# Two units of the first projection take turns over the token tiles while the norm goes on

## The chip, the cores and the metric

One NeuronCore of a Trainium2 chip runs the whole computation in one launch. The metric is the device time of one execution in microseconds. All work is in 32-bit floating point; a product of two such matrices is made of three matmuls of halves (high times high, high times low, low times high), which is why every weight and activation is split into a high and a low part.

## The reference, cut to what matters

Two layers over 1024 latent tokens and 256 context tokens (T = 1280), 1024 channels each. What concerns the change is the beginning of a layer:

```python
mod_x = (silu_c @ w_ada[l] + b_ada[l])[:, None, :]        # likewise mod_c from c_ctx
sh1_x, sc1_x, gt1_x, sh2_x, sc2_x, gt2_x = jnp.split(mod_x, 6, axis=-1)
hx = modulate(rms_norm(x, g_norm1[l]), sh1_x, sc1_x)      # likewise hc from ctx
qa, ka, va, qb, kb, vb, qc, kc, vc = jnp.split(hx @ w_in[l], bounds, axis=-1)
# then: QK norm of every head, rotary positions on q and k of groups A and C,
# three kinds of attention, output projection with gate gt1, ConvFFN with sh2, sc2 and gate gt2
```

`rms_norm` divides a token by the root of its mean square and multiplies by a gain; `modulate(h, shift, scale)` is `h * (1 + scale) + shift`. The modulation vectors of a layer are six pieces of 1024; the kernel makes them in three pieces of 2048 columns.

## The kernel before, in words

Activations lie with channels on the partitions: eight tiles X[k] of 128 channels by 1280 tokens. Instructions are issued in an order written out by hand in Python generators; each engine works through its own part of that order, and semaphores hold it where an operand is not there yet. The order of the program is therefore also the order of each engine's queue, and of the DMA queue of SyncE, which loads weights and tables.

The first norm of a layer (`FirstNorm`) goes over the tokens in five pieces of 256. A piece needs its sum of squares (`squares`, in layer 1 the loop `last`), a statistics step (`norm_stat`: TensorE sums over the channels at L226, VectorE adds the epsilon at L229, GpSimd takes the power at L230), a cast (`norm_cast`, L237: TensorE spreads the factor over 128 partitions), and eight steps of `norm_apply`, one for each X[k]: VectorE scales (L255), ScalarE writes the high part (L274, or L271 and L272), VectorE or GpSimd the low part (L263 or L260). `SPREAD` and `SPREAD1` say which steps give the low part to GpSimd.

The projection `inproj` has six units of 384 columns (two of kind A, two of C, two of B) and, in each unit, ten tiles of 128 tokens: 60 slots. It runs unit 0 over all ten tiles, then unit 1, and so on. In slot s:

- `stage1(s)`: 24 matmuls into `acc` (L398), ScalarE's square of the result (L403), the copy of v (L407), VectorE's sum over each head (L413, L415), GpSimd's power (L416);
- `stage2(s-1)`: VectorE multiplies by the root (L430), GpSimd multiplies by the cosine table or the gain (L440, L445), VectorE by the sine table (L445);
- the rotary add of slot s-2 (L452), and `stage3(s-2)`: TensorE's transposes into `pt` (L463, L465), ScalarE's and VectorE's copies into `sg` (L472, L474, L475), DMA to memory (L478).

Ahead of each slot stands `bg(s)`. In slots 0 to 7 it issues squares and norm steps (counts in `Q_ST`, `P_ST`, `P_ST1`), enough that the piece a slot reads is complete; `STAT0`, `CAST0` and their like place statistics and casts behind a slot's matmuls. At slot 8 it closes the norm's buffers and sets up the remaining modulation pieces (three in layer 0, two in layer 1), whose weights (L1370) go into the space of X[k], free once the norm has read it; the pieces run from slot 9 on, two small steps every second slot (`hold`). From slot `S_FIRST` on, the first operands of the attention are loaded and cast (`attention_first`, L513 and on).

A unit's weights are four raw loads of 384 KB (`load`, L348), each split into high (ScalarE, L103) and low (VectorE, L104) by `split`. Four raw buffers and six split buffers exist; `split(n)` also issues the load n + 4. `weights` splits the next unit's first two in its slots 2 and 4 of ten, `weights_done` the other two behind the last slot.

Of the kernel before, what the change touches and what calls it, by code (L numbers as in the profile page):

```python
# [14 lines left out]
F32 = mybir.dt.float32  # L15
F32R = mybir.dt.float32r
# [7 lines left out]
KT = D // 128  # L24
# [3 lines left out]
CH = [(0, 512), (512, 512), (1024, 256)]  # L28
NP = 8
NPT = 6  # L30
Q_PRE = [0, 0, 0, 2, 4, 3, 1, 1]
Q_ST = [1, 2, 4, 3, 0, 2, 0, 1, 0]
SQ_ENG = "vgv"
STAT0 = [0, 3, 3]
CAST0 = [1, 3, 4]
STAT1 = [0]
CAST1 = [1, 3, 5]
SPREAD = "vgvvgvvv"
SPREAD1 = "gvvvgvvv"
TST = [0, 0, 0, 0, 0, 0, 0, 0, 0, 0, 0, 0, 0, 0, 0, 0, 0, 2, 1, 0, 0, 0, 0, 1, 1, 0]  # L40
# [1 line left out]
T_CAST = [16, 17]  # L42
T_TAB = 10
T_SP = [0, 1, 1, 1]
P_ST1 = [4, 4, 4, 4, 4, 4, 4, 4]
P_ST = [1, 7, 1, 7, 5, 2, 5, 4]
STRETCH = 1.2
LEADL = 35
LEADB = 12
# [24 lines left out]
class Build:  # L74
# [126 lines left out]
    def squares(self, X, ss, sqp):  # L201

        nc = self.nc
        n = self.squared = 0
        for o in (512, 768, 1024):
            dst = ss[:, o - 512:o - 256]
            for k in range(KT):
                x = X[k][:, o:o + 256]
                if k == 0:
                    nc.scalar.activation(dst, x, AF.Square)  # L210
                else:
                    sq = sqp[:, 256 * (n % 2):256 * (n % 2) + 256]
                    n += 1
                    nc.scalar.activation(sq, x, AF.Square)
                    (nc.vector if SQ_ENG[o // 256 - 2] == "v" else nc.gpsimd).tensor_tensor(dst, dst, sq, op=ALU.add)
                self.squared += 1
                yield
# [93 lines left out]
    def ip_tables(self, l):  # L311

        nc, i = self.nc, self.i
        tp = self.iptab[1]
        self.ip_gains = gains = tp.tile([128, 320], F32, name=self.name("gains"))
        nc.sync.dma_start(gains[:], i["gains"][:, l, :])
        self.ip_tabs = {}  # L320
        for kd, off in (("A", 0), ("C", 256)):
            gd = GD[kd]
            h = gd // 2
            self.ip_tabs[kd] = cc, ss = [tp.tile([128, 2, 8, gd], F32, name=self.name(z + kd)) for z in ("cos", "sin")]
            for z, w in ((cc, "cos"), (ss, "sin")):
                nc.sync.dma_start(z[:, 1], i[w + kd][:])
            yield
            if kd == "A":
                for a, b in (("A", 0), ("B", 128), ("C", 256)):
                    z = gains[:, b + GD[a]:b + 2 * GD[a]]  # L330
                    nc.gpsimd.tensor_scalar(z, z, -math.sqrt(GD[a]), 1.0, op0=ALU.mult, op1=ALU.mult)
            g = gains[:, off:off + 2 * gd].rearrange("p (j d) -> p j d", d=gd)
            for j in range(2):
                nc.gpsimd.tensor_tensor(cc[:, j], cc[:, 1], g[:, j, :].unsqueeze(1).to_broadcast([128, 8, gd]), op=ALU.mult)
                for x, y in ((0, h), (h, 0)):
                    nc.gpsimd.tensor_tensor(ss[:, j, :, x:x + h], ss[:, 1, :, x:x + h],
                                            g[:, j, y:y + h].unsqueeze(1).to_broadcast([128, 8, h]), op=ALU.mult)
            yield

    def ip_loads(self, l):  # L340

        nc, i = self.nc, self.i
        raw, wts = {}, {}

        def load(n):
            if n < 24:
                w = self.ipraw[1].tile([128, 2, 384], F32, name=self.name("ipr"), tag="ipr", bufs=4)
                nc.sync.dma_start(w[:], i["win"][l, n // 4, :, 2 * (n % 4):2 * (n % 4) + 2, :])  # L348
                raw[n] = w

        def split(n):
            if n < 24:
                hi = self.ipw[1].tile([128, 2, 384], F32R, name=self.name("iph"), tag="iph", bufs=6)
                lo = self.ipw[1].tile([128, 2, 384], F32R, name=self.name("ipl"), tag="ipl", bufs=6)
                self.split(hi[:], lo[:], raw.pop(n)[:])
                wts[n] = (hi, lo)
                load(n + 4)

        def weights(u, t):
            if t in (2, 4):  # L360
                split(4 * u + 3 + t // 2)
            return [wts[4 * u + j] for j in range(4)]

        def weights_done(u):
            split(4 * u + 6)
            split(4 * u + 7)

        for j in range(4):
            load(j)
        self.ip_weights, self.ip_weights_done = weights, weights_done  # L370

        return split

    def inproj(self, l, H, bg, stat):
# [2 lines left out]
        tmpl = self.pool("iptmp")  # L377
        tmp, psp = tmpl[1], self.ipps[1]
        gains, tabs = self.ip_gains, self.ip_tabs
        slots = [(u, t) for u in range(6) for t in range(10)]  # L380
        state, vst = {}, {}

        def stage1(s):
# [8 lines left out]
            ws = self.ip_weights(u, t)  # L392
# [9 lines left out]
            sq = tmp.tile([128, 320], F32, name=self.name("sq"), tag="sq", bufs=1)  # L402
            nc.scalar.activation(sq[:, g0 * gd:W], acc[:, g0 * gd:W], AF.Square)  # L403
            nv = NV[kd]
            if t % 5 == 0:
                vst[u] = tmp.tile([128, 2, 5, 64], F32, name=self.name("vst"), tag="vst", bufs=2)
            nc.scalar.copy(vst[u][:, :nv, t % 5, :], acc[:, W:384].rearrange("p (v d) -> p v d", d=64))  # L407
            if t % 5 == 4:
                for j in range(nv):
                    dst = self.vs[l][self.vidx(u, j)][:, 64 * (t - 4):64 * (t - 4) + 320]  # L410
                    nc.scalar.dma_start(dst.rearrange("p (t d) -> p t d", d=64), vst[u][:, j, :, :])
            ss = tmp.tile([128, 8], F32, name=self.name("ss"), tag="ss", bufs=3)
            nc.vector.tensor_reduce(ss[:, g0:ng], sq[:, g0 * gd:W].rearrange("p (g d) -> p g d", d=gd), axis=AX.X,  # L413
                                    op=ALU.add)
            nc.vector.tensor_scalar(ss[:, g0:ng], ss[:, g0:ng], gd * EPS, None, op0=ALU.add)  # L415
# [39 lines left out]
        def stage3(s):  # L455
# [10 lines left out]
            qs = self.qs[l][u]  # L466

            def put(r, nb, src, c):
                sg = tmp.tile([128, 2, nb, 128], F32R, name=self.name("sg"), tag=f"sg{nb}", bufs=nb)
                hi, lo = (sg[:r, z].rearrange("p b n -> p (b n)") for z in range(2))  # L470
                if kd == "A":
                    nc.scalar.copy(f32(hi), src)  # L472
                else:
# [11 lines left out]
        for s in range(len(slots) + 2):  # L485
# [7 lines left out]
                stage3(s - 2)  # L493
            if 1 <= s <= len(slots):
                stage2(s - 1)
        self.close(tmpl, self.ipraw, self.iptab, self.ipw, self.ipps)

    @staticmethod
    def vidx(u, j):
# [636 lines left out]
    def run(self):  # L1136
# [19 lines left out]
        ss0 = sqp[1].tile([128, 512], F32, name="ss0")  # L1156
        ss = sqp[1].tile([128, 768], F32, name="ss")
        sqt = self.pool("sqt")
        squares = self.squares(X, ss, ss0)
# [33 lines left out]
        for l in range(L):  # L1193
# [12 lines left out]

            n_w = iter(range(1000))
            adw = lambda n_w=n_w: self.slot(f"x{next(n_w) % KT}")
            todo, hold = deque(), [True]
            first = self.attention_first(l)  # L1210
            lam = self.lambdas() if l == 0 else iter(())

            def bg(s, l=l, norm=norm, adw=adw, todo=todo, hold=hold, sqp=sqp, nps=nps, lam=lam, first=first, tables=tables):
                if s < 8:
                    nq, np_ = Q_ST[s] if l == 0 else 0, (P_ST, P_ST1)[l][s]
                    for j in range(max(nq, np_)):
                        if j < nq:
                            next(squares, None)
                        if j < np_:
                            norm.step()  # L1220
                    while norm.done < KT * (s // 2 + 1):
                        norm.step()
                elif s == 8:
                    self.close(sqp, self.ntl, nps)
                    which = [(a, b) for a, b in ((l, 1), (l, 2), (l + 1, 0)) if a < L]
                    loads = AdaLoads(self, adw, which, 1)
                    todo.extend(self.ada(a, b, loads, self.ipps[1]) for a, b in which)
                if s in (12, 16):
                    next(lam, None)
# [43 lines left out]
            def last(unit, spare, l=l, X=X, H=H, out=out):  # L1273
# [388 lines left out]
```

## Time and profile before

| what | value |
|---|---|
| runs shown | 3519.92, 3525.55 and 3526.09 us, median 3525.55 us |
| the profiled execution | 3518.43 us, span of its instructions 3516.7 us |
| TensorE busy in the span | 3381.2 us (96%) |
| VectorE, ScalarE, GpSimd busy | 2049.2, 1383.7 and 960.1 us |
| mean granted clock of TensorE | 0.988 |
| matmuls of the projection, layer 0 | from 38.0 us; slot 59 ends at 376.4 us |
| matmuls of the projection, layer 1 | from 1921.7 us; slot 59 ends at 2227.8 us |

Times in rows of the timeline are microseconds from the first instruction. A row gives start, duration, engine, line, operation, written and read tiles, shapes and count; in brackets stands how long the engine had been idle before it and what ended that. Matmuls overlap each other, so the duration of one is longer than the distance to the next. Rows with the letter q behind the engine (SPq, ACTq) are DMA instructions that the engine issues.

### The profile page before, as it was taken

Reading aid. Unit: us, or ns where it says so; the run is one execution under the profiler, and the core shown is the slowest. Engines: PE = TensorE matmul, PEld = TensorE weight load, DVE = VectorE, ACT = ScalarE, POOL = GpSimd, SP = SyncE. Lnnn points to the kernel's source line nnn. Section 1 sums busy time; section 2 is a strip of 40 time slices with the busy share of each in tenths; the row PEclk is TensorE's granted clock in tenths of the full one; section 3 lists DMA queues with packets and bytes.
Section 4 is the critical chain, followed back from the end, with each engine's and each line's share of the span. In section 5 each row is a group of like instructions: output and inputs, shape, how many; then the busy total and the mean of one; then the engine's idle time right before and its main releaser. Section 6 shows DMA issues by size and latency. Waiting matters only on the chain.

```text
span 3516.7 us, 55261 instructions
## 1 busy us (share of the span) xinstructions
PE 3381.2 (96%) x21808; PEld 2914.1 (83%) x21808; DVE 2049.2 (58%) x4167; ACT 1383.7 (39%) x2412; POOL 960.1 (27%) x863
## 2 busy tenths in 40 slices
PE   5899899999999999999999899999999999999999
PEld 3789788888888888888887789888888888888887
DVE  5544578776565544445446544587775645555555
ACT  4322478777332221122223322478775322222211
POOL 3444467755100000000002344467763100000000
PEclk8999999999999999999999999999999999999999
DMA  5563611220211111111112453512212111111112
GB/s 210 197 234 108 158 43 46 68 62 2 92 52 36 37 43 41 38 42 37 37 36 98 145 178 107 146 48 63 60 36 68 47 48 54 42 48 54 43 50 76
DMA packets 138084, 266.59 MB, mean 76 GB/s; under 512 B 15200, under 2 KB 76128, under 8 KB 137824
## 3 DMA queue, kind: packets, MB, share of 16 engines
q1 hardware_dynamic: 76880, 230.27, 21.1%
q10 hardware_dynamic: 60944, 32.78, 3.1%
q8 instruction: 172, 2.82, 0.3%
q14 instruction: 88, 0.72, 0.1%
HBM read 222.09 MB, written 40.89 MB: 75 GB/s over the span
## 4 chain that ended last, share of the span: by engine, by line
PE 83%; DVE 7%; POOL 4%; DMA 2%; issue 2%; ACT 2%; ACTq 0%; SPq 0%; DVEq 0%; POOLq 0%
PE psu L999 15%; PE psg L999 15%; PE dacc L1086 15%; PE acc L398 11%; PE T L783 6%; PE T L802 6%; PE S L676 5%; PE acc L935 4%; DVE P L694 2%; PE T L676 2%; POOL P L755 1%; PE ada L166 1%; POOL P L754 1%; DVE hl L263 1%; PE pt L463 1%
## 5 line engine op out<-in xcount | busy, mean ns | idle before, releaser
L1093 DVE SCALAR_TENSOR_TENSOR x<-dacc,mods,x 128x512 f32<-128x512 f32 (+1 forms) x440 | 303.8, 696 | 474.9 <-PE dacc L1086 474.8
L1086 PE MATMUL dacc<-ah,w 128*128 128x512 f32 (+1 forms) x1760 | 530.4, 369 | 2.1 <-DVE x L1093 1.6
L999 PE MATMUL psu<-hh,w 128*128 128x512 f32 (+1 forms) x1760 | 516.5, 368 | 1.1 <-ACT hh L274 1.1
L999 PE MATMUL psg<-hh,w 128*128 128x512 f32 (+1 forms) x1760 | 516.4, 368 | 0.0
L719 ACT ACTIVATE P<-P,sm 128x1280 f32<-128x1280 f32 (+3 forms) x360 | 434.6, 1209 | 122.0 <-DVE sm L694 99.8
L103 ACT CAST w<-wr 128x1024 fp32r<-128x1024 f32 x138 | 144.1, 1044 | 726.5 <-PE psg L999 538.5
L1086 PEld LDWEIGHTS dacc<-ah,w 128*128 128x128 f32 x1760 | 322.2, 188 | 61.1 <-DVE x L1093 4.5
L999 PEld LDWEIGHTS psu<-hh,w 128*128 128x128 f32 x1760 | 321.4, 189 | 56.5 <-ACT hh L274 1.3
L999 PEld LDWEIGHTS psg<-hh,w 128*128 128x128 f32 x1760 | 321.4, 189 | 55.5
L694 DVE CUSTOM_DVE_ANT_0 P<-S,small,sm 128x1024 f32<-128x1024 f32 x256 | 328.5, 1283 | 32.9 <-PE S L676 18.9
L398 PE MATMUL acc<-iph,hh 128*128 128x384 f32 (+1 forms) x960 | 334.6, 349 | 5.8 <-ACT iph L103 3.9
L398 PE MATMUL acc<-iph,hl 128*128 128x384 f32 (+1 forms) x960 | 323.4, 337 | 9.0 <-DVE hl L263 5.3
L999 PE MATMUL psu<-hl,w 128*128 128x512 f32 (+1 forms) x880 | 324.7, 369 | 0.1
L1086 PE MATMUL dacc<-al,w 128*128 128x512 f32 (+1 forms) x880 | 324.6, 369 | 0.0
L398 PE MATMUL acc<-ipl,hh 128*128 128x384 f32 (+1 forms) x960 | 323.0, 336 | 1.1 <-DVE ipl L104 1.1
L999 PE MATMUL psg<-hl,w 128*128 128x512 f32 (+1 forms) x880 | 324.0, 368 | 0.0
L783 PE MATMUL T<-ident,P 128*128 128x128 f32 x2400 | 313.5, 274 | 5.9 <-POOL P L755 5.5
L783 PEld LDWEIGHTS T<-ident,P 128*128 128x128 f32 x2400 | 270.8, 141 | 37.3 <-POOL P L755 12.0
L728 POOL TENSOR_SCALAR P<-P,sm 128x1280 f32<-128x1280 f32 (+3 forms) x216 | 248.1, 1151 | 181.4 <-DVE sm L726 116.7
L802 PE MATMUL T<-PT,v 128*64 128x128 f32 x4800 | 293.8, 276 | 3.5 <-DVE sm L836 3.0
L802 PEld LDWEIGHTS T<-PT,v 128*64 128x64 f32 x4800 | 259.6, 137 | 33.7 <-issue 14.7
L788 ACT COPY PT<-T 128x512 f32<-128x512 f32 (+1 forms) x461 | 246.7, 584 | 71.4 <-PE T L783 69.2
(195 smaller groups left out, 5612.9 us busy)
## 6 DMA issues: line engine op xcount, KB each, us to landing
wr<-in_wup SPq DMA_DIRECT2D x88, 512.0 KB, 3.5
x<-in_wada SPq DMA_DIRECT2D x80, 512.0 KB, 6.3
qs<-sg ACTq DMA_DIRECT2D x180, 128.0 KB, 1.8
wr<-in_wdown SPq DMA_DIRECT2D x44, 512.0 KB, 3.5
ipr<-in_win SPq DMA_DIRECT2D x48, 384.0 KB, 3.8
v<-vs SPq DMA_DIRECT2D x30, 320.0 KB, 3.2
hh<-qs SPq DMA_DIRECT2D x26, 320.0 KB, 6.2
x<-in_x SPq DMA_DIRECT2D x32, 256.0 KB, 4.4
```

Of the source, the lines that this page charges most:

```text
L103: self.nc.scalar.copy(hi, raw)
L398: nc.tensor.matmul(acc[:, c0:], lhsT=a[:, o:o + 128], rhs=b[:, k % 2, c0:], start=(k == 0 and a is hi and b is wh), stop=(k == KT - 1 and ...
L676: nc.tensor.matmul(S[:, pc:pc + w], lhsT=q[:K, 128 * t:128 * t + 128], rhs=k[:K, k0:k0 + w], start=(j == 0), stop=(j == len(ks) - 1))
L694: nc.vector.tensor_tensor_reduce(P[:, o:o + n], S[:, base:base + n], tab, op0=ALU.add, op1=ALU.min, scale=1.0, scalar=start, accum_out=sm[ ...
L719: nc.scalar.activation(P[:, :n], P[:, :n], AF.Exp, bias=sm[:, 0:1], scale=-1.0, accum_out=at())
L728: lambda e: nc.gpsimd.tensor_scalar(P[:, :n], P[:, :n], sm[:, 3:4], 1.0, op0=ALU.mult, op1=ALU.mult),
L783: nc.tensor.transpose(tp[:, 256 * x + 128 * hs:256 * x + 128 * hs + 128], P[hs][:, col[kt]:col[kt] + 128], self.ident[:])
L788: nc.scalar.copy(ts[:, :w], tp[:, :w])
L802: nc.tensor.matmul(O[64 * hs:64 * hs + 64, :128], lhsT=hds[hs]["v"][:, kt, :], rhs=ts[:, x + 128 * hs:x + 128 * hs + 128], start=(kt == kt ...
L999: nc.tensor.matmul(ps[:, o:o + n], lhsT=a[:, 128 * k:128 * k + 128], rhs=b, start=(k == 0 and a is wh and b is hi), stop=(k == KT - 1 and ...
L1086: nc.tensor.matmul(acc, lhsT=a[:, off:off + 128], rhs=b[:, o:o + n], start=(kk == 0 and a is wh and b is hi), stop=(kk == 1 and a is wl))
L1093: nc.vector.scalar_tensor_tensor(xs, acc, self.mods[l][:, 40 + m, v:v + 1], xs, op0=ALU.mult, op1=ALU.add)
```

## The change

Units 0 and 1 are in use at once. The first 20 slots alternate in pairs of token tiles:

`(0,0) (0,1) (0,2) (0,3) (1,0) (1,1) (0,4) (0,5) (1,2) (1,3) (0,6) (0,7) (1,4) (1,5) (0,8) (0,9) (1,6) (1,7) (1,8) (1,9)`

as (unit, token tile); units 2 to 5 follow as before. The five pieces of the norm are first read in slots 0, 2, 6, 10 and 14, where they were first read in slots 0, 2, 4, 6 and 8.

- The norm steps are spread over slots 0 to 13 (`S_NORM` = 14); the squares of layer 0 are nearly all issued beside the slots (three ahead of slot 0, 21 in slots 0 to 8; before, 11 ahead and 13 beside). Their scratch is the read part of X[0] and X[1].
- Unit 1's weights are split in slots 1 to 4, unit 2's in slots 16 to 19, the others at the old places. Eight split buffers for six; two raw buffers and, for weights 2 and 3, two more in a pool that is closed after their split; `split(n)` issues the load n + 2.
- The other modulation pieces are set up in slot 19 (`S_ADA`): the first load goes out in slot 20, the first matmuls stand in slot 24.
- The rotary table of kind C gets its own pool; it is loaded in slot 17 and multiplied by the gains in slot 20 (before: 9 and 14). The lambda loads go from slot 12 to 14.
- Units 0 and 1 share the tile that gathers v; `ss` has two buffers for three; `sg` tiles are merged.
- Ahead of layer 1 the four weight loads are issued behind the table loads, not ahead of them.

```diff
-Q_PRE = [0, 0, 0, 2, 4, 3, 1, 1]
-Q_ST = [1, 2, 4, 3, 0, 2, 0, 1, 0]
+S_NORM = 14
+S_ADA = 19
+Q_PRE = [0, 0, 0, 0, 0, 1, 1, 1]
+Q_ST = [1, 2, 2, 3, 3, 2, 2, 3, 3, 0, 0, 0, 0, 0]
-STAT0 = [0, 3, 3]
-CAST0 = [1, 3, 4]
+STAT0 = [2, 5, 9]
+CAST0 = [3, 6, 10]
-CAST1 = [1, 3, 5]
+CAST1 = [1, 5, 9]
-P_ST1 = [4, 4, 4, 4, 4, 4, 4, 4]
-P_ST = [1, 7, 1, 7, 5, 2, 5, 4]
+P_ST1 = [4, 4, 2, 2, 2, 2, 2, 2, 2, 2, 2, 2, 2, 2]
+P_ST = [3, 5, 0, 0, 4, 4, 0, 2, 3, 3, 0, 2, 3, 3]
...
-                    sq = sqp[:, 256 * (n % 2):256 * (n % 2) + 256]
+                    sq = X[n % 2][:, :256]
...
+            if kd == "C":
+                self.iptabc = self.pool("iptabc", side="right")
+                tp = self.iptabc[1]
...
-                w = self.ipraw[1].tile([128, 2, 384], F32, name=self.name("ipr"), tag="ipr", bufs=4)
+                pool = self.ipfirst if n in (2, 3) else self.ipraw
+                w = pool[1].tile([128, 2, 384], F32, name=self.name("ipr"), tag="ipr", bufs=2)
...
-                hi = self.ipw[1].tile([128, 2, 384], F32R, name=self.name("iph"), tag="iph", bufs=6)
-                lo = self.ipw[1].tile([128, 2, 384], F32R, name=self.name("ipl"), tag="ipl", bufs=6)
+                hi = self.ipw[1].tile([128, 2, 384], F32R, name=self.name("iph"), tag="iph", bufs=8)
+                lo = self.ipw[1].tile([128, 2, 384], F32R, name=self.name("ipl"), tag="ipl", bufs=8)
...
-                load(n + 4)
-
-        def weights(u, t):
-            if t in (2, 4):
+                if n > 1:
+                    load(n + 2)
+                if n == 3:
+                    self.close(self.ipfirst)
+
+        def weights(s, u, t):
+            if s in (1, 2, 3, 4):
+                split(3 + s)
+            elif s in (16, 17, 18, 19):
+                split(s - 8)
+            elif u > 1 and t in (2, 4):
                 split(4 * u + 3 + t // 2)
...
         def weights_done(u):
-            split(4 * u + 6)
-            split(4 * u + 7)
+            if u > 1:
+                split(4 * u + 6)
+                split(4 * u + 7)
...
-        slots = [(u, t) for u in range(6) for t in range(10)]
+        slots = self.ip_slots
...
-            if t % 5 == 0:
-                vst[u] = tmp.tile([128, 2, 5, 64], F32, name=self.name("vst"), tag="vst", bufs=2)
+            both, v0 = (0, u) if u < 2 else (u, 0)
+            if t % 5 == 0 and u != 1:
+                vst[both, t // 5] = tmp.tile([128, 2, 5, 64], F32, name=self.name("vst"), tag="vst", bufs=2)
...
+                if kd == "A" and nb == 1:
+                    sg = tmp.tile([128, 1, 1, 128], F32R, name=self.name("sg"), tag="sg1", bufs=1)
+                else:
+                    sg = tmp.tile([128, 2, 2, 128], F32R, name=self.name("sg"), tag="sg2", bufs=2)[:, :, :nb]
...
+        two = [(0, 0), (0, 2), (1, 0), (0, 4), (1, 2), (0, 6), (1, 4), (0, 8), (1, 6), (1, 8)]
+        return [(u, t + j) for u, t in two for j in range(2)] + [(u, t) for u in range(2, 6) for t in range(10)]
...
-                if s < 8:
+                if s < S_NORM:
...
-                    while norm.done < KT * (s // 2 + 1):
+                    while norm.done < KT * (max(t for _, t in self.ip_slots[:s + 1]) // 2 + 1):
                         norm.step()
-                elif s == 8:
+                elif s == S_NORM:
                     self.close(sqp, self.ntl, nps)
+                elif s == S_ADA:
                     which = [(a, b) for a, b in ((l, 1), (l, 2), (l + 1, 0)) if a < L]
...
-                if s in (12, 16):
+                if s in (14, 16):
                     next(lam, None)
-                if s in (9, 14):
+                if s in (17, 20):
                     next(tables, None)
                 if todo and hold[0]:
-                    hold[0] = 0
+                    hold[0] -= 1
                     return
                 steps = 2
                 while todo:
                     if steps <= 0:
-                        hold[0] = not r
+                        hold[0] = 3 if s < S_ADA + 3 else 0 if r else 1
                         return
...
-                out["split"] = self.ip_loads(l + 1)
                 tables = self.ip_tables(l + 1)
...
+                self.ipfirst = self.pool("ipfirst", side="right")
+                out["split"] = self.ip_loads(l + 1)
```

More of the change, by code (lines that the diff above doesn't have):

```diff
@@ L199, in norm_sq, with squares @@
             (eng or nc.gpsimd).tensor_tensor(ss, ss, sq[:, :n], op=ALU.add)
-    def squares(self, X, ss, sqp):
+    def squares(self, X, ss):
         nc = self.nc
@@ L391, in stage1 @@
             o = 128 * t
-            ws = self.ip_weights(u, t)
+            ws = self.ip_weights(s, u, t)
             acc = psp.tile([128, 384], F32, name=self.name("acc"), tag="acc", bufs=3)
@@ L404, in stage1 @@
             nv = NV[kd]
-            if t % 5 == 0:
-                vst[u] = tmp.tile([128, 2, 5, 64], F32, name=self.name("vst"), tag="vst", bufs=2)
-            nc.scalar.copy(vst[u][:, :nv, t % 5, :], acc[:, W:384].rearrange("p (v d) -> p v d", d=64))
+            both, v0 = (0, u) if u < 2 else (u, 0)
+            if t % 5 == 0 and u != 1:
+                vst[both, t // 5] = tmp.tile([128, 2, 5, 64], F32, name=self.name("vst"), tag="vst", bufs=2)
+            vt = vst[both, t // 5]
+            nc.scalar.copy(vt[:, v0:v0 + nv, t % 5, :], acc[:, W:384].rearrange("p (v d) -> p v d", d=64))
             if t % 5 == 4:
@@ L410, in stage1 @@
                     dst = self.vs[l][self.vidx(u, j)][:, 64 * (t - 4):64 * (t - 4) + 320]
-                    nc.scalar.dma_start(dst.rearrange("p (t d) -> p t d", d=64), vst[u][:, j, :, :])
-            ss = tmp.tile([128, 8], F32, name=self.name("ss"), tag="ss", bufs=3)
+                    nc.scalar.dma_start(dst.rearrange("p (t d) -> p t d", d=64), vt[:, v0 + j, :, :])
+            ss = tmp.tile([128, 8], F32, name=self.name("ss"), tag="ss", bufs=2)
             nc.vector.tensor_reduce(ss[:, g0:ng], sq[:, g0 * gd:W].rearrange("p (g d) -> p g d", d=gd), axis=AX.X,
@@ L468, in put @@
             def put(r, nb, src, c):
-                sg = tmp.tile([128, 2, nb, 128], F32R, name=self.name("sg"), tag=f"sg{nb}", bufs=nb)
-                hi, lo = (sg[:r, z].rearrange("p b n -> p (b n)") for z in range(2))
+                if kd == "A" and nb == 1:
+                    sg = tmp.tile([128, 1, 1, 128], F32R, name=self.name("sg"), tag="sg1", bufs=1)
+                else:
+                    sg = tmp.tile([128, 2, 2, 128], F32R, name=self.name("sg"), tag="sg2", bufs=2)[:, :, :nb]
+                hi, lo = (sg[:r, z].rearrange("p b n -> p (b n)") for z in (0, sg.shape[1] - 1))
                 if kd == "A":
@@ L495, in inproj, with ip_slots @@
                 stage2(s - 1)
-        self.close(tmpl, self.ipraw, self.iptab, self.ipw, self.ipps)
+        self.close(tmpl, self.iptabc, self.ipraw, self.iptab, self.ipw, self.ipps)
+    @property
+    def ip_slots(self):
+        two = [(0, 0), (0, 2), (1, 0), (0, 4), (1, 2), (0, 6), (1, 4), (0, 8), (1, 6), (1, 8)]
+        return [(u, t + j) for u, t in two for j in range(2)] + [(u, t) for u in range(2, 6) for t in range(10)]
     @staticmethod
@@ L1155, in run @@
         sqp = self.pool("sqp", side="right")
-        ss0 = sqp[1].tile([128, 512], F32, name="ss0")
         ss = sqp[1].tile([128, 768], F32, name="ss")
         sqt = self.pool("sqt")
-        squares = self.squares(X, ss, ss0)
+        ss0 = sqt[1].tile([128, 512], F32, name="ss0")
+        squares = self.squares(X, ss)
         early = iter(f"h{z}{k}" for _ in range(2) for k in range(KT) for z in "hl")
@@ L1208, in run @@
             adw = lambda n_w=n_w: self.slot(f"x{next(n_w) % KT}")
-            todo, hold = deque(), [True]
+            todo, hold = deque(), [1]
             first = self.attention_first(l)
@@ L1288, in last @@
                 out["ss"] = ss = sqp[1].tile([128, 768], F32, name=self.name("ss"))
+                self.ipfirst = self.pool("ipfirst", side="right")
+                out["split"] = self.ip_loads(l + 1)
                 ss0, sqs = spare[0][:, :512], [spare[1][:, :512], spare[1][:, 512:1024]]
```

## The prediction, made before the changed kernel ran

> **What bounds the kernel now.** I read the page first, then who TensorE waits for around the first projection, then the timeline of the two places where a projection starts, engine by engine.
>
> ```profile
> span 3516.7 us, 55261 instructions
> PE 3381.2 (96%) x21808; PEld 2914.1 (83%) x21808; DVE 2049.2 (58%) x4167; ACT 1383.7 (39%) x2412; POOL 960.1 (27%) x863
> ```
>
> TensorE is busy for 3381.2 of 3516.7 us. The change adds and removes no matmul, so it can only win from the 135.5 us in which TensorE does nothing, and from matmuls that ran at a reduced clock.
>
> ```profile
> PE nst L226 <- DVE ss L215: 10.2, 1, 10.2
> PE ada L166 <- DMA x<-in_wada: 6.3, 1, 6.3
> PE acc L398 <- DVE hl L263: 5.3, 3, 2.5
> PE pt L463 <- DVE y L452: 4.1, 4, 1.8
> ...
> 132.50 0.38 PE L463 MATMUL pt<-ident,y 128*128 128x128 f32 x2
> ...
> 136.99 0.38 PE L463 MATMUL pt<-ident,y 128*128 128x128 f32 x2
> ...
> 54.29 0.42 ACT L403 ACTIVATE sq<-acc 128x320 f32<-128x320 f32 x1
> ...
> 181.92 0.44 ACT L403 ACTIVATE sq<-acc 128x320 f32<-128x320 f32 x1 [1.24 <-PE acc L398]
> ...
> 1935.25 0.44 ACT L403 ACTIVATE sq<-acc 128x320 f32<-128x320 f32 x1 [1.11 <-PE acc L398]
> ...
> 2049.49 0.23 ACT L403 ACTIVATE sq<-acc 128x64 f32<-128x64 f32 x1 [1.24 <-PE acc L398]
> ...
> 148.43 1.90 PE L166 MATMUL ada<-x,sil 128*2 128x512 f32 x16
> ```
>
> The first four rows are TensorE's waits from 35 to 320 us. Between two transposes (132.50 and 136.99) lies one undisturbed slot of unit 0 or 1: 4.49 us. ScalarE's square (L403) marks the end of a slot's matmuls. In layer 0, slots 0 to 19 end at 54.29 and 181.92, 127.6 us for 19 slots that need 85.3 us by themselves. Modulation matmuls stand in five of those slots (1.90 us each) with one set of transposes, 10.5 us with their small gaps; 31 us are lost. In layer 1, slots 1 to 19 take 114.2 us where 18 slots need 80.8 and modulation 10.5: 23 us lost. So some 54 us at most lie within this change's reach.
>
> The larger part is lost because VectorE sets the pace:
>
> ```profile
> 108.50 0.47 DVE L413 TENSOR_REDUCE ss<-sq 128x5 f32<-128x320 f32 x1
> ...
> 111.43 0.49 DVE L452 TENSOR_TENSOR y<-y,m 128x320 f32<-128x320 f32 x1 [1.13 <-POOL y L445]
> 111.84 0.48 DVE L413 TENSOR_REDUCE ss<-sq 128x5 f32<-128x320 f32 x1
> ...
> 1935.72 0.49 DVE L413 TENSOR_REDUCE ss<-sq 128x5 f32<-128x320 f32 x1 [0.95 <-ACT sq L403]
> ...
> 1943.39 0.48 DVE L413 TENSOR_REDUCE ss<-sq 128x5 f32<-128x320 f32 x1
> ...
> 1950.00 0.47 DVE L413 TENSOR_REDUCE ss<-sq 128x5 f32<-128x320 f32 x1
> ```
>
> In VectorE's order a slot's own work runs from its reduction (L413) to the rotary add of the slot before (L452), and behind that stand the norm steps, squares and weight split of the next slot, ahead of the next reduction. TensorE's transpose (L463) waits for that add. Without any norm step the cycle is 3.34 us to the next reduction (108.50 to 111.84), 3.42 to the add's end; I take 3.45. With four norm steps it is 6.61 (1943.39 to 1950.00), so a step costs 0.79. With four steps and a split it is 7.67 (1935.72 to 1943.39), so a split costs 1.06. A slot takes the longer of 4.49 and 3.45 plus what is put into it. About one step is free in a slot, or one split; four steps are not.
>
> **The change part by part.** Fewer norm steps per slot. Eight slots held the 32 steps; now fourteen do, since two units take turns and a new 256-token piece is due only every fourth slot after the first four. VectorE's work is the same. The gain is that more slots' own work runs beside it.
>
> Layer 1, worked through. Slots 0 and 1 hold four steps each as before; the split of weight 4 moves into slot 1, so its reduction goes from 1935.72 to 1936.8. To the reduction of slot 13: 12 x 3.45 = 41.4, 24 steps x 0.79 = 19.0, three splits (slots 2 to 4) 3.2, and the loss of slot 4, below, 3.2: 66.8, at 2003.6. From there the last add, a transpose and slots 15 to 19 at 4.49 are 3.45 + 0.4 + 22.5 = 26.3, so slot 19 ends at 2029.9. Before it ended at 2049.49, or 2039.0 without the modulation that now comes later. Gain 9.1 us. The splits of slots 16 to 19 give 3.45 + 1.06 = 4.51, hidden.
>
> The new stall, slot 4. It is the first of unit 1, and its last weight is split in slot 4 itself, behind slot 4's norm steps on VectorE. By the cycle above, the reduction of slot 2 starts at 1942.9, and TensorE starts slot 4 at 1946.8 and has weights for 18 of 24 matmuls, 3.1 us; VectorE ends that split at 1955.1. TensorE stands some 5 us, runs the last six at a reduced clock (1.9 us, pitch below), and the next reduction comes 2.6 us after VectorE is free; 0.6 more for slot 5 on the reduced clock. Between nothing (the split gets ahead) and 6 us a layer; I take 3.2.
>
> Layer 0 before its slot 2:
>
> ```profile
> 47.62 2.00 DVE L215 TENSOR_TENSOR ss<-ss,ss 128x256 f32<-128x256 f32 x4
> ...
> 49.93 0.95 DVE L215 TENSOR_TENSOR ss<-ss,ss 128x256 f32<-128x256 f32 x2
> ...
> 51.19 2.25 DVE L263 SCALAR_TENSOR_TENSOR hl<-x,mods,hh 128x256 fp32r<-128x256 f32 x3
> ...
> 54.73 0.49 DVE L413 TENSOR_REDUCE ss<-sq 128x5 f32<-128x320 f32 x1 [0.51 <-ACT sq L403]
> ```
>
> Ahead of slot 0 stood 11 squares, seven with an add on VectorE; now three, two with an add. Five adds of 0.49 are 2.5 us, and ScalarE's share, on which the low parts waited, about 1: piece 0, done at 53.44, comes at 49.9 (2.5 to 5 earlier). Then three steps and a square (2.9), slot 0's reduction (0.7), five steps, two squares and a split (6.0): the reduction of slot 1 at 59.5. To slot 13: 41.4 + 24 steps 19.0 + nine adds on VectorE 4.5 + three splits 3.2 + slot 4 3.2 + a wait of the statistics' matmul (L226) for the last square in slot 2, 1.0 + slots 6 and 10, which TensorE sets, 1.0 = 73.3. With the same 26.3, slot 19 ends at 159.1, against 181.92 - 10.5 = 171.4. Gain 12.3 us. The 10.2 us wait of L226 in slot 3 is in this: seven steps and three squares stood ahead of it; the later two sums now end a slot or more ahead.
>
> Modulation from slot 20.
>
> ```profile
> 124.27 3.50 PE L166 MATMUL ada<-x,sil 128*2 128x512 f32 x8 [6.26 <-DMA x<-in_wada]
> ...
> 1993.29 2.99 PE L166 MATMUL ada<-x,sil 128*2 128x512 f32 x8 [6.18 <-DMA x<-in_wada]
> ...
> 137.19 0.44 ACT L403 ACTIVATE sq<-acc 128x320 f32<-128x320 f32 x1 [2.98 <-DMA qs<-sg]
> ...
> 142.01 0.33 SPq L348 DMA_DIRECT2D ipr<-in_win  x1
> ...
> 116.76 1.19 SPq L348 DMA_DIRECT2D ipr<-in_win  x2
> ...
> 118.00 4.68 SPq L1370 DMA_DIRECT2D x<-in_wada  x6
> ```
>
> The stall of 6.2 us in each layer is the second modulation weight: its load stood on SyncE's queue behind weight loads that waited for splits (116.76), went out at 118.00 and was there at 124.27, 6.3 us later. Now the first load goes out in slot 20 and its matmul stands in slot 24, so the first is hidden. The second is issued in slot 24's place of the queue, behind one weight load that waits for the split of slot 22. Such a split freed the queue 4.8 us after the end of the slot before (137.19 to 142.01), 0.4 us after slot 22 then. It needs 6.3 us, less about 1 with one load ahead and not two: 5.7 after slot 22. TensorE asks for it one slot, a transpose and the first weight's matmuls later, 5.3. I take 1.5 us a layer (0 to 6.3). The matmuls themselves (three pieces in layer 0, two in layer 1) only move. By the hold counts the last piece ends in slot 50 of layer 0, and the attention's first loads and casts go from slots 45-51 to 50-56, still ahead of slot 60: nothing.
>
> ```profile
> 152.25 1.13 POOL L336 TENSOR_TENSOR sinC<-sinC,gains 128x128 f32<-128x128 f32 x2
> ```
>
> The rotary table of unit 2 is now made in slot 20, ahead of that slot's power on GpSimd: six products, two of which took 1.13, about 3.4 us. Between nothing, where GpSimd idles in a slot of 4.49, and 3.4 a layer; GpSimd is busy 27% of the span, so I take 0.25 a layer. Fewer raw weights in flight (two and two for four), the shared value tile, one buffer less for ss, and smaller sg tiles: each next use is two slots or more away, 9 us, so I cost them at nothing. In the last stage before layer 1 the loads only change places on a queue with tens of us to spare.
>
> Sum: layer 0 12.3 - 1.5 - 0.25 = 10.5, layer 1 9.1 - 1.5 - 0.25 = 7.4; together 18 us. The profiled execution took 3518.4 us, the runs shown 3519.9 to 3526.1; the four have a mean of 3522.5. Less 18 that is 3504.5, 3500.4 against the profiled one alone.
>
> **The rivals.** *More is won.* The split of slot 4 hides (3.2 in each layer), the second load lands in time (1.5 in each), and the start gains 5, not 3.5: 11 more, 29 in all, 3493. For it: ScalarE has room. Against: VectorE's order is fixed, and the split stands behind the steps.
>
> *The stalls only move.* The second modulation load comes as late as before (6.3, and some 2 of slow matmuls, in each layer, 13.6 more) and slot 0 gains nothing of its 3.5: about 1 us is left, 3521. For it: the queue is as blocked in slot 22 as it was in slot 9. Against: one weight load ahead, not two, and four slots of lead for the first.
>
> *Slower: the clock.*
>
> ```profile
> 1947.37 0.44 PE L463 MATMUL pt<-ident,y 128*128 128x128 f32 x2 [2.59 <-DVE y L452]
> ...
> 54.97 0.52 PE L398 MATMUL acc<-ipl,hh 128*128 128x384 f32 x1
> 55.29 0.52 PE L398 MATMUL acc<-iph,hl 128*128 128x384 f32 x1
> ...
> 57.20 0.34 PE L398 MATMUL acc<-iph,hl 128*128 128x384 f32 x1
> 57.37 0.34 PE L398 MATMUL acc<-iph,hh 128*128 128x384 f32 x1
> ...
> 74.00:78.00 4.00, 0.00 (x0) 0.53 0.00 0
> ...
> 110.00:114.00 4.00, 2.63 (x17) 1.00 0.08 20
> ...
> 1945.00:1950.00 5.00, 2.63 (x12) 0.82 0.20 71
> ```
>
> (The last three are stretches: TensorE's busy time and count, then the granted clock.) After an idle stretch a matmul starts every 0.32 us, not every 0.17, and a slot's 24 need 7.7 us. A wait of 2.59 us lowered the clock (0.82); 1.4 us idle from 110 to 114 left it at 1.00. After the change TensorE waits in nearly every slot from 2 to 13 for 0.5 to 1 us. If these small waits were enough, each such slot would cost 7.7 for about 5, 2.7 more: seven of the 24 slots take the whole 18, ten make the kernel slower by 9, 3531.
>
> The Trainium skill, "TensorE: Matmul & The Clock Gate", names both sides: by its section on the warmup an idle window of about 3.4 us halves the clock; by "A second HAM failure mode: psum-queue depth-cycling", frequent micro-idles between groups of matmuls can make the gate swing too. By the first rule the small waits cost nothing and the sum stands; by the second it is this rival, 3531. The trace lies nearer the first, though here 2.59 us was enough.
>
> **How the numbers follow.** My forecast, 10 to 26 us won, has 0.55; more 0.20; stalls that move 0.14; slower 0.11. About 7 us, 0.2%, is what a measurement of this kernel can tell from no change. Forecast and more are faster, and 0.02 of the third case; 0.01 of the last is too small to tell: faster 0.77, same 0.13, slower 0.10. The likeliest is 3504, its own range 3494 to 3513. For the whole I take 3488 to 3521: the upper end takes in the stalls that move, the lower the larger gain with runs like the profiled one; the slower rival is left out above.
>
> **What would show it.** Reductions (L413) in slots 5 to 13 of layer 1 about 5.0 us apart, not 6.6; slot 19 of layer 1 near 2019 (2029.9 less what layer 0 gives); a TensorE wait of about 5 us for the last split (L104) in slot 4 of both layers; the 10.2 us wait of L226 gone; modulation's first wait 0 to 3 us. It is wrong if a granted clock under 0.9 stands in slots 6 to 13, if slots 5 to 13 stay over 6 us apart, or if the second modulation load is as late as before.

## The result, and the profile after

The changed kernel takes 3501.59 us (median of 4 runs, 3500.61 to 3503.31), the kernel before 3524.05 us (median of 4, 3519.92 to 3526.09). The ratio is 0.9941 with a 95% interval of 0.9929 to 0.9952: 17 to 25 us faster. The two profiled executions differ by 16.5 us in their spans, since the one of before lies at the fast end of its runs. The working of the prediction is held against these two.

The changed kernel's page, and TensorE's waits from 35 to 320 us (total, times, longest):

```profile
span 3500.2 us, 55407 instructions
PE 3381.1 (97%) x21808; PEld 2915.1 (83%) x21808; DVE 2046.2 (58%) x4167; ACT 1384.7 (40%) x2412; POOL 960.0 (27%) x863
...
PE pt L482 <- DVE y L471: 6.9, 6, 1.8
PE acc L415 <- ACT iph L105: 4.6, 1, 4.6
PE acc L415 <- POOL hl L265: 3.6, 1, 3.6
PE nst L231 <- DVE ss L220: 2.7, 1, 2.7
...
PE ada L168 <- DMA x<-in_wada: 2.4, 2, 1.9
```

TensorE's busy time is the same to 0.1 us; all of the difference is time in which it did nothing. The waits for statistics (10.2) and for the modulation load (6.3) have shrunk to 2.7 and 2.4, and a new one stands second: 4.6 us for a weight's high part. Lines have moved: ScalarE's square that marks a slot's end is L420, the transposes L482 and L484, VectorE's reduction L432 and its rotary add L471.

The ends of slots 0 and 19 in layer 0, and of slots 1 and 19 in layer 1:

```profile
51.83 0.42 ACT L420 ACTIVATE sq<-acc 128x320 f32<-128x320 f32 x1
...
160.79 0.44 ACT L420 ACTIVATE sq<-acc 128x320 f32<-128x320 f32 x1 [1.62 <-PE acc L415]
...
1925.41 0.44 ACT L420 ACTIVATE sq<-acc 128x320 f32<-128x320 f32 x1 [0.44 <-PE acc L415]
...
2022.81 0.23 ACT L420 ACTIVATE sq<-acc 128x64 f32<-128x64 f32 x1 [1.76 <-PE acc L415]
```

Slot 19 of layer 0 ends 21.1 us earlier than before, but 10.5 us of modulation still have to come; by slot 59 8.4 us are left (368.02 for 376.44). In layer 1 slots 1 to 19 take 97.4 us for 114.2, and slots 0 to 59 291.3 for 297.2: 5.9 us. The two projections give 14.3 us of the 16.5. The other 2 lie in the stretch between the projections and behind the second, where the change does nothing that I can name; over all kernels below, the stretch between them varies from 1551.1 to 1555.4 us without a pattern. I leave that part open.

Slot 4 of layer 1, on four engines:

```profile
1943.55 0.51 ACT L279 ACTIVATE hh<-x,mods 128x256 fp32r<-128x256 f32 x1 [2.40 <-DVE x L260]
...
1943.96 0.81 ACT L105 CAST iph<-ipr 128x768 fp32r<-128x768 f32 x1
1944.81 0.96 DVE L106 TENSOR_TENSOR ipl<-ipr,iph 128x768 fp32r<-128x768 f32 x1 [0.51 <-ACT iph L105]
1944.83 0.45 PE L415 MATMUL acc<-iph,hh 128*128 128x384 f32 x1 [4.42 <-ACT iph L105]
1945.82 0.69 PE L415 MATMUL acc<-ipl,hh 128*128 128x384 f32 x1 [0.55 <-DVE ipl L106]
```

TensorE waits 4.42 us for the high part of weight 7 and 0.55 for the low one. ScalarE could not cast earlier: the norm's high part stood ahead of it and waited 2.40 us for VectorE. In layer 0 the two waits are 4.55 and 0.58.

Slot 24 of layer 0 (SyncE's weight load, its modulation loads, TensorE's modulation matmuls, and the ends of slots 23 and 24):

```profile
174.90 0.33 SPq L357 DMA_DIRECT2D ipr<-in_win  x1
175.29 7.48 SPq L1401 DMA_DIRECT2D x<-in_wada  x6
178.88 0.39 ACT L420 ACTIVATE sq<-acc 128x256 f32<-128x256 f32 x1 [3.59 <-PE acc L415]
...
181.89 1.03 PE L168 MATMUL ada<-x,sil 128*2 128x512 f32 x4 [1.85 <-DMA x<-in_wada]
...
183.45 1.03 PE L168 MATMUL ada<-x,sil 128*2 128x512 f32 x4 [0.54 <-DMA x<-in_wada]
...
188.87 0.38 ACT L420 ACTIVATE sq<-acc 128x256 f32<-128x256 f32 x1 [7.28 <-PE acc L415]
```

The second modulation load goes out behind the weight load, 0.8 us after slot 22 (174.47), and arrives 6.6 us later. The slot takes 9.99 us where one with two modulation weights takes 6.4. In layer 1 it takes 8.76.

### The profile page after: what moved, and what is told of

The parts are those of the page before. It is cut to its first block, busy times and chain, and to the rows that moved or that the text cites. A ratio compares the mean times of both kernels' runs of the same rounds, so it can differ in the third digit from the quotient of the medians.

```text
span 3500.2 us, 55407 instructions
## 1 busy us (share of the span) xinstructions
PE 3381.1 (97%) x21808; PEld 2915.1 (83%) x21808; DVE 2046.2 (58%) x4167; ACT 1384.7 (40%) x2412; POOL 960.0 (27%) x863
## 3 DMA queue, kind: packets, MB, share of 16 engines
q1 hardware_dynamic: 76880, 230.27, 21.1%
## 4 chain that ended last, share of the span: by engine, by line
PE 81%; DVE 7%; POOL 4%; issue 2%; DMA 2%; ACT 2%; ACTq 0%; SPq 0%; POOLq 0%; DVEq 0%
PE psu L1027 16%; PE psg L1027 16%; PE dacc L1114 15%; PE acc L415 10%; PE T L811 6%; PE T L830 6%; PE acc L963 5%; PE S L704 4%; DVE P L722 2%; PE T L704 2%; POOL P L783 1%; PE ada L168 1%; POOL P L782 1%; POOL y L464 1%; PE pt L482 1%
## 5 line engine op out<-in xcount | busy, mean ns | idle before, releaser
L722 DVE CUSTOM_DVE_ANT_0 P<-S,small,sm 128x1024 f32<-128x1024 f32 x256 | 328.5, 1283 | 34.7 <-PE S L704 21.1
```

What stands on the lines that cost most here:

```text
L722: nc.vector.tensor_tensor_reduce(P[:, o:o + n], S[:, base:base + n], tab, op0=ALU.add, op1=ALU.min, scale=1.0, scalar=start, accum_out=sm[ ...
```

## The experiments

Each kernel was timed beside the kernel before, and the ratio is to that; spans and slots come from one profiled execution each. Slots that kernels have alike can still differ between profiles: slots 1 to 19 of layer 1, 97.4 us in the changed kernel, take 96.1 and 97.3 in two kernels below that leave them as they are (two loads ahead, and eleven squares ahead).

| kernel | median us | ratio (95%) | span of profile | layer 0, slot 59 ends | layer 1, slots 0 to 59 |
|---|---|---|---|---|---|
| before | 3524.05 | | 3516.7 | 376.4 | 297.2 |
| changed | 3501.59 | 0.9941 (0.9929 to 0.9952) | 3500.2 | 368.0 | 291.3 |
| late modulation alone | 3508.3 | 0.9968 (0.9956 to 0.998) | 3505.7 | 369.9 | 291.7 |
| changed, weight 7 split in slot 3 | 3496.21 | 0.9931 (0.9919 to 0.9944) | 3497.3 | 367.9 | 287.3 |
| changed, two loads ahead | 3500.51 | 0.9942 (0.993 to 0.9955) | 3498.6 | 366.0 | 292.8 |
| changed, layer 1's norm in 8 slots | 3504.47 | 0.9956 (0.9943 to 0.9968) | 3502.7 | 365.5 | 295.6 |
| changed, modulation from slot 15 | 3499.51 | 0.993 (0.9916 to 0.9943) | 3498.5 | 367.7 | 288.3 |
| two loads, shared sg tile | 3496.08 | 0.9921 (0.9907 to 0.9934) | 3493.2 | 364.0 | 288.2 |
| two loads, shared sg tile, early split | 3491.91 | 0.9911 (0.9897 to 0.9925) | 3490.4 | 363.7 | 284.5 |
| order of before, late modulation, two loads, shared sg tile | 3501.46 | 0.9944 (0.993 to 0.9957) | 3498.9 | 368.1 | 287.9 |

**Late modulation alone.** The kernel before, with the pieces set up in slot 19 and the same pauses:

```diff
                 elif s == 8:
                     self.close(sqp, self.ntl, nps)
+                elif s == 19:
                     which = [(a, b) for a, b in ((l, 1), (l, 2), (l + 1, 0)) if a < L]
...
-                        hold[0] = not r
+                        hold[0] = 3 if s < 22 else 0 if r else 1
```

> The kernel before, with one thing of the change: the modulation pieces are set up in slot 19 (first load in slot 20, first matmuls in slot 24), the units one after the other and the norm in eight slots as before. Theory A (VectorE's cycle and the modulation stall each give a part): slot 10 loses its stall, 9.4 us in layer 0 and 8.3 in layer 1 over an undisturbed slot with modulation, and slot 24 gets about the 3.6 and 2.3 us that the changed kernel shows there: 11 to 12 us faster than before, and slots 2 to 7 of layer 1 stay 6.6 us apart or more. Rival B (the turns of the two units alone give the gain, a later modulation only moves its stall): within 3 us of before, with a wait of 5 to 6 us for the second modulation load in slot 24 of each layer.

Its page's span, and the ends of slots 19, 23 and 24 of layer 0 and slots 1 and 19 of layer 1:

```profile
span 3505.7 us, 55275 instructions
...
162.94 0.44 ACT L403 ACTIVATE sq<-acc 128x320 f32<-128x320 f32 x1 [0.89 <-PE acc L398]
...
180.81 0.39 ACT L403 ACTIVATE sq<-acc 128x256 f32<-128x256 f32 x1 [3.57 <-PE acc L398]
190.71 0.38 ACT L403 ACTIVATE sq<-acc 128x256 f32<-128x256 f32 x1 [7.06 <-PE acc L398]
...
1928.67 0.44 ACT L403 ACTIVATE sq<-acc 128x320 f32<-128x320 f32 x1 [0.65 <-PE acc L398]
...
2025.29 0.23 ACT L403 ACTIVATE sq<-acc 128x64 f32<-128x64 f32 x1 [0.99 <-PE acc L398]
```

The span is 11.0 us shorter, theory A's 11 to 12; rival B falls. Slot 10 takes 4.49 us in both layers, and slot 24 9.90 and 8.53, as in the changed kernel. In the projections this edit alone gives 6.6 and 5.5 us, 12.1 of the changed kernel's 14.3 (0.8 of it stands ahead of the end of slot 0 in layer 0, where the edit does nothing). By the runs the share is smaller: 0.0032 of 0.0059, about 11 of 21 us, and the two intervals do not overlap, so the rest of the change does win something (about 9 us by the runs, 5.5 by the spans, 2.2 to be seen in the projections). Slots 1 to 19 of layer 1 take 96.6 us here, no more than the changed kernel's 97.4: turns and spread norm won nothing to be seen there. So the question was where their gain had gone.

**The split of weight 7, a slot earlier.** In the changed kernel:

```diff
-            if s in (1, 2, 3, 4):
+            if s in (1, 2, 3):
                 split(3 + s)
+                if s == 3:
+                    split(7)
```

> The changed kernel, with the last split of unit 1 (weight 7) in slot 3 behind that of weight 6 instead of in slot 4 behind slot 4's norm steps. Theory A: the wait of 4.4 to 5.1 us in slot 4 goes in both layers, and slots 4 and 5 lose their matmuls at half clock; VectorE carries the same work, so 2 to 4 us a layer, 4 to 8 in all, faster than the changed kernel. Rival B (the wait is one of VectorE's total work up to slot 4 and comes back as a wait for the rotary add): under 2 us in all.

Slots 1 and 19 of layer 1 end here:

```profile
1927.71 0.44 ACT L422 ACTIVATE sq<-acc 128x320 f32<-128x320 f32 x1 [1.19 <-PE acc L417]
...
2020.24 0.23 ACT L422 ACTIVATE sq<-acc 128x64 f32<-128x64 f32 x1 [1.76 <-PE acc L417]
```

Slots 1 to 19 of layer 1 take 92.5 us, 4.9 less than in the changed kernel and 3.6 less than with the same slots at 96.1: at or above the upper end of the 2 to 4 expected. In layer 0 slots 0 to 19 take 107.8 for 109.0, only 1.2 less: slot 4 is 3.6 shorter, but 1.6 comes back in slot 6, behind a wait of 3.3 us of the statistics' matmul for the last square on GpSimd, and 1.6 in slot 10. The last is no longer wait: TensorE stands for the same 1.84 us there in both kernels, but in this one the granted clock falls behind it. Those two waits, each with a stretch behind it (TensorE's busy time, count and granted clock), first in the changed kernel, then in this one:

```profile
110.31 0.41 PE L482 MATMUL pt<-ident,y 128*128 128x128 f32 x2 [1.84 <-DVE y L471]
110.00:115.00 5.00, 4.69 (x29) 1.00 0.15 42
...
108.28 0.41 PE L484 MATMUL pt<-ident,y 128*128 128x128 f32 x2 [1.84 <-DVE y L473]
108.00:113.00 5.00, 4.72 (x19) 0.66 0.15 42
```

In layer 0 rival B is nearly right, in layer 1 theory A. The whole, 0.9931, is 3.5 us under the changed kernel, which the intervals do not separate; the projections are 4.1 us shorter. This is where much of the turns' gain had gone.

**Two modulation weights loaded ahead.**

```diff
-        while self.todo and len(self.ready) <= min(self.ahead, self.got):
+        while self.todo and len(self.ready) <= self.ahead:
```

> The changed kernel, with two modulation weights loaded ahead from the first request of a piece (four DMAs in slot 20 instead of two), so that the second is not queued behind the weight load of slot 22. Theory A: the stall in slot 24 (2.4 and 1.2 us idle, 3.6 and 2.3 us with its slow matmuls) goes: 4 to 6 us faster than the changed kernel. Rival B (the DMA engines are full, the load would be late anyway): slot 24 keeps its wait, within 1 us of the changed kernel.

Each expectation is half right. Slot 24 loses its stall (6.41 and 6.43 us), as theory A says, yet the ratio stays, 0.9942, as rival B says for another reason. The time comes back in slots 21 to 23, 15.2 us in layer 0 (13.6 in the changed kernel) and 17.2 in layer 1 (13.4). There ScalarE waits (SyncE's loads, ScalarE's store and its next copy into the same buffer):

```profile
161.14 3.48 SPq L1401 DMA_DIRECT2D x<-in_wada  x4
...
162.50 0.45 ACTq L500 DMA_DIRECT2D qs<-sg  x1
...
170.53 0.26 ACT L494 COPY sg<-pt 64x128 f32<-64x128 f32 x1 [4.80 <-DMA qs<-sg]
```

A store of 32 KB, issued 1.4 us after the start of 2 MB of loads, keeps its buffer for 8.0 us. The 64-row piece of kind A has one buffer, so ScalarE stands 4.8 us, and everything behind it, the square of slot 21 first, stands too. The next store of this size, issued at 170.82 us as the last of these loads came in, landed in 1.8 us. The Trainium skill says under "Trainium Kernel Development and Optimization", Key Constraints, that DMAs issued from the queues of SyncE, ScalarE and GpSimd run on the same 16 DMA engines and interleave; the trace agrees, and here the small store took as long as the loads beside it (5.4 to 7.6 us). That the loads are what held it is read from these durations; no run takes them away and leaves the rest.

**The norm of layer 1 in eight slots.** The units still take turns:

```diff
-CAST1 = [1, 5, 9]
+CAST1 = [1, 3, 5]
-P_ST1 = [4, 4, 2, 2, 2, 2, 2, 2, 2, 2, 2, 2, 2, 2]
+P_ST1 = [4, 4, 4, 4, 4, 4, 4, 4, 0, 0, 0, 0, 0, 0]
```

> The changed kernel, with layer 1's norm steps four in each of slots 0 to 7 and none in slots 8 to 13 (casts behind slots 1, 3 and 5), so that the units take turns but the norm is not spread. Theory A (a slot takes the longer of 4.49 us and 3.45 plus 0.79 for each norm step): slots 5 to 7 of layer 1 6.6 us apart, slots 8 to 13 4.5: 12 x 5.0 = 60 us become 6 x 6.6 + 6 x 4.5 = 67, so 5 to 7 us slower than the changed kernel, all in layer 1. Rival B (the norm's total VectorE work counts, not how it is spread): within 2 us.

VectorE's reductions, first in this kernel (slots with four steps, then with none), then in the changed one (slots with two):

```profile
1957.46 0.48 DVE L432 TENSOR_REDUCE ss<-sq 128x5 f32<-128x320 f32 x1
1964.14 0.47 DVE L432 TENSOR_REDUCE ss<-sq 128x5 f32<-128x320 f32 x1
...
1984.19 0.49 DVE L432 TENSOR_REDUCE ss<-sq 128x5 f32<-128x320 f32 x1 [0.98 <-ACT sq L420]
1988.71 0.49 DVE L432 TENSOR_REDUCE ss<-sq 128x5 f32<-128x320 f32 x1 [1.00 <-ACT sq L420]
```

```profile
1965.52 0.48 DVE L432 TENSOR_REDUCE ss<-sq 128x5 f32<-128x320 f32 x1
1970.84 0.49 DVE L432 TENSOR_REDUCE ss<-sq 128x5 f32<-128x320 f32 x1
1975.84 0.48 DVE L432 TENSOR_REDUCE ss<-sq 128x5 f32<-128x320 f32 x1
```

The rule for a slot nearly holds: 6.68 with four steps, 4.52 with none (there VectorE waits for the square, so TensorE sets the pace), 5.32 and 5.00 with two. But slots 1 to 19 lose only 2.1 us (99.5 for 97.4; 3.4 against the same slots at 96.1), not 5 to 7. The changed kernel's slots 6 to 13 are 0.22 longer than the rule's 5.03 on the mean, slots 6 and 10, each behind a cast, the longest (5.66), and slot 5 catches up with slot 4's stall (6.55). By the runs the kernel is about 5 us slower than the changed one (0.9956 for 0.9941), as theory A expects, but the intervals overlap, and 1.8 of the 4.3 us that layer 1 is longer by slot 59 lie past slot 19, where the edit does nothing. Spreading the norm is worth 2 to 3.4 us in the slots of layer 1 that it touches, less than theory A; between rival B's 2 and theory A's 5 the runs do not decide.

**Modulation right behind the norm.**

```diff
                 elif s == S_NORM:
                     self.close(sqp, self.ntl, nps)
-                elif s == S_ADA:
                     which = [(a, b) for a, b in ((l, 1), (l, 2), (l + 1, 0)) if a < L]
...
-                        hold[0] = 3 if s < S_ADA + 3 else 0 if r else 1
+                        hold[0] = 0 if r else 1
```

> The changed kernel, with the modulation pieces set up in slot 14, right behind the norm, and no pause after the first load: first load in slot 15, first matmuls in slot 16. No weight load stands on SyncE's queue between slots 4 and 16, so the second load is not held up by one. Theory A (the wait was the queue's order): no wait of TensorE for a modulation load over 1 us, slot 24 like its neighbours; 4 to 6 us faster than the changed kernel. Rival C (whenever the first three weights come, 3 MB in one go, the stores of sg wait behind them on the DMA engines, and units 0 and 1 have one buffer for the 64-row piece): slots 15 to 18 lose 3 us or more in each layer and the total stays within 2 us of the changed kernel.

TensorE waits for no modulation load in the projections any more; with the kernel of two loads ahead, where the stall went too, that shows the queue's order as the cause of slot 24's stall. Layer 1 gains 3.0 us by slot 59 (288.3 for 291.3), layer 0 0.3: there ScalarE waits for stores, as this row of its waits from 100 to 200 us shows (3.6 us in two waits in the changed kernel).

```profile
ACT sg L494 <- DMA qs<-sg: 13.7, 6, 3.6
```

The whole, 0.993, is 2.1 us under the changed kernel by medians, which the intervals do not separate. Rival C names the right mechanism for layer 0, in other slots than expected (14, 15, 21 and 22 above all); for layer 1 theory A holds.

**Two loads and two buffers.** The 64-row piece goes into the free half of the slot's own tile of two:

```diff
-                if kd == "A" and nb == 1:
-                    sg = tmp.tile([128, 1, 1, 128], F32R, name=self.name("sg"), tag="sg1", bufs=1)
-                else:
-                    sg = tmp.tile([128, 2, 2, 128], F32R, name=self.name("sg"), tag="sg2", bufs=2)[:, :, :nb]
+                sg = sgt[:, 1:, :1] if kd == "A" and nb == 1 else sgt[:, :, :nb]
```

> The kernel with two modulation weights loaded ahead in slot 20, and the 64-row piece of kind A put into the free half of its slot's double-buffered sg tile, so that ScalarE no longer waits for one single buffer's store. In the kernel with two loads ahead, slot 24 lost its stall but slots 21 to 23 took 15.2 and 17.2 us for 13.2. Rival C: slots 21 to 23 go back to 13.5 or less in both layers and slot 24 stays at 6.4, so 4 to 6 us faster than with two loads alone and than the changed kernel. Theory D (the stores themselves are late whatever the buffers, and two buffers run full as well): slots 21 to 23 stay over 14.5, within 1.5 us of the two loads alone.

Rival C holds: slots 21 to 23 take 13.6 and 13.0 us, slot 24 6.41 in both, and the ratio falls from 0.9942 to 0.9921; slots 0 to 59 of layer 1 are 4.6 us shorter than with two loads alone. ScalarE's wait for that store is down to 0.8 us (100 to 200 us):

```profile
ACT sg L493 <- DMA qs<-sg: 0.8, 1, 0.8
```

**All three.** Early split, two loads, shared tile.

> The kernel with two loads ahead and the shared sg tile, and weight 7 split in slot 3. If the parts add: 5 us for the split (layer 0 about 1, layer 1 about 4) on top of the kernel with two loads and the shared tile; against the kernel before 29 to 33 us faster. If rival C is wrong, about 27.

0.9911, 32 us faster by the medians than the kernel before, which took 3523.85 us beside it: within the noise the parts add (3.5 us more than without the early split, for 5 expected). It is the fastest kernel here; its interval (0.9897 to 0.9925) lies below the changed kernel's.

**The same mends in the order of before.** What the turns are worth once their stall is gone:

> The kernel before (units one after the other, norm in eight slots) with the late modulation, the two loads ahead and the shared sg tile: what is left out against the kernel with all three is the turns of the two units, the spread norm and the squares. Theory A (a slot takes the longer of 4.49 us and 3.45 plus its norm steps): slots 1 to 19 as in the kernel with the late modulation alone (109.5 us in layer 0, 96.6 in layer 1 against 108.3 and 92.5 with turns and an early split), slot 24 at 6.4: 3 to 5 us faster than the late modulation alone, and 8 to 11 us slower than all together, 3500 to 3503. Rival F (the turns give nothing once the loads and stores are mended): within 3 us of all together, about 3493.

0.9944 against 0.9911: the turns, the spread norm and the squares together are worth 0.0033, about 12 us by the runs and 8.5 by the spans, once the split, the loads and the store no longer hold the slots; 7.8 of it stand in the projections, 2.9 of these ahead of the end of slot 0. In the change as made, 2.2 us of that were to be seen in the projections. The early split belongs to it: against the kernel with two loads and the shared tile alone, slots 1 to 19 of layer 1 are 0.7 us longer here, against all three 4.2. Rival F falls. Against the late modulation alone the mends win 6.8 us, more than the 3 to 5 expected. No run takes the turns, the spread and the squares apart from each other in both layers.

**Eleven squares ahead of slot 0.** One run, with its profile.

```diff
-Q_PRE = [0, 0, 0, 0, 0, 1, 1, 1]
-Q_ST = [1, 2, 2, 3, 3, 2, 2, 3, 3, 0, 0, 0, 0, 0]
+Q_PRE = [0, 0, 0, 2, 4, 3, 1, 1]
+Q_ST = [0, 0, 0, 0, 3, 2, 2, 3, 3, 0, 0, 0, 0, 0]
```

> The changed kernel, with 11 squares ahead of slot 0 in layer 0 as in the kernel before (13 in slots 4 to 8) instead of three. Theory A (VectorE is the pace up to slot 13, and its total work is the same): slot 0 ends 2 to 3 us later than in the changed kernel's 51.83, the statistics' wait of slot 2 (2.7 us) goes, and slot 3 ends within 1 us of 69.40, slot 19 within 1 us of 160.79. Rival E (the early start of slot 0 is a gain of its own): slot 19 2 to 3 us later.

Slots 0, 3 and 19 of layer 0 in it, for 51.83, 69.40 and 160.79:

```profile
54.56 0.42 ACT L420 ACTIVATE sq<-acc 128x320 f32<-128x320 f32 x1
...
69.91 0.44 ACT L420 ACTIVATE sq<-acc 128x320 f32<-128x320 f32 x1 [2.73 <-PE acc L415]
...
162.00 0.44 ACT L420 ACTIVATE sq<-acc 128x320 f32<-128x320 f32 x1 [1.65 <-PE acc L415]
```

Slot 0 ends 2.7 us later, slot 3 0.5, slot 19 1.2. About 0.9 of the last is the clock: here too it falls behind slot 10's wait of 1.83 us, so that slot 10 takes 5.20 us for 3.66 and slot 11 0.6 less. Most of the early start is given back by slot 3: theory A, on one run.

## Why the prediction was right, step by step

The total was right: 18 us forecast against the profiled execution, 16.5 measured, and 21 by the ratio of the runs. The terms were less good. Of the 16.5 only 14.3 lie in the two projections, where the whole 18 were forecast, so that the last 2 us of the agreement are luck.

- *Slot 4's new stall.* Forecast some 5 us, then six matmuls at a reduced clock; 5.0 in layer 1 and 5.1 in layer 0. The cause was half right: ScalarE's cast is late first, VectorE's low part adds 0.55.
- *The slot rule.* Forecast 66.8 us from slot 1 to slot 13 of layer 1; the slots' ends lie 70.8 apart. The step that failed is the size of a slot with two norm steps (5.25 on the mean of slots 6 to 13, not 5.03) and of what follows the stall (6.55 in slot 5), as the fourth experiment shows. Layer 1's 9.1 us were 6.3 (103.7 without modulation, then 97.4).
- *Layer 0's start.* 2.5 us earlier, not 3.5; the wait of statistics in slot 2 2.7, not 1.0, with a clock of 0.71 from 65 to 70 us behind it, for which the sum had no term. Slot 19 came at 160.79 for 159.1.
- *Slot 24.* 1.5 us a layer forecast; 3.6 and 2.3 with the slow matmuls. The mechanism, a load held on the queue by a weight load, is shown by the kernels that loaded two ahead and that set modulation up in slot 14.
- *What carries the gain.* Here the text misled: it called VectorE's pace the larger part of the loss and named the spread of the norm as the gain. That loss is real, but the change removed little of it. The first experiment shows that 12.1 of the 14.3 us in the projections, and 11 of 21 by the runs, come from the modulation's move, which takes 11.5 us out of slot 10 in layer 0 and 10.3 in layer 1 (4.49 for 15.95, 4.49 for 14.83, each with 2.0 of matmuls that come later). By counting all slots to the nineteenth together, the sum held that stall without naming it, and so came out right.
- *The clock rival.* It did not come in the changed kernel. TensorE's busy time, count and granted clock in four stretches of layer 1 of the changed kernel:

```profile
1940.00:1945.00 5.00, 0.58 (x4) 1.00 0.38 104
1945.00:1950.00 5.00, 4.45 (x15) 0.52 0.31 91
...
1960.00:1965.00 5.00, 4.61 (x28) 1.00 0.22 67
...
1980.00:1985.00 5.00, 4.14 (x24) 1.00 0.14 36
```

After the 4.4 us of slot 4 the clock falls to 0.52; small waits in slots 6 to 13 of both layers leave it at 1.00. But it was nearer than the forecast had it: in three of the eight kernels with turns (early split, all three, eleven squares ahead) the clock fell behind the 1.84 us wait in slot 10 of layer 0 and cost about 1 us, and in the other five the same wait left it at 1.00. By the rule of the Trainium skill, "TensorE: Matmul & The Clock Gate", Part 1, an idle window of about 3.4 us halves the clock; the 4.4 us of slot 4 agree, while the 1.84 us lie under that figure, and there the measurement decides.
- *The stalls only move.* This rival was right on the place (slot 24) and wrong on the size, 5.9 us in both layers for 17.8 before (slot 10 less 6.5 us).

## What to carry to other kernels

Before crediting a reordering, count separately what each stall in its stretch costs, and test the smallest part alone: here a later start of the modulation, with the units and the norm as they were, gave over half of the gain. A step put behind background work on a shared engine becomes the new stall where it is needed in the same slot, and a load waits as long as whatever stands ahead of it in its queue. A burst of loads lengthens small stores, so a single store buffer can give back what an earlier load won.

## What I had not expected of the hardware

A 32 KB store held its buffer for 8.0 us beside 2 MB of loads, where the next one, in the same kernel, landed in 1.8 us. And the length of a wait alone does not tell whether TensorE's clock falls. It fell to 0.82 behind 2.59 us without work in the kernel before, and stayed at 1.00 behind 2.58 us in slot 4 of layer 1 in the kernel with the early split (its transpose, then the stretch around it):

```profile
1946.02 0.44 PE L484 MATMUL pt<-ident,y 128*128 128x128 f32 x2 [2.58 <-DVE y L473]
...
1945.00:1950.00 5.00, 3.98 (x24) 1.00 0.21 63
```

In slot 10 of layer 0, 1.84 us did either. So the prediction's premise that 2.59 us lowers the clock is one of two outcomes; what decides between them no run here shows.
